# Products with tokens on partitions: 512 weight columns per matmul in place of 256, and another split of the PSUM banks

## The chip, the cores and the metric

The kernel runs on one core of a Trainium2 chip. The metric is the device time of one execution in microseconds. The kernel before took 967.45 us, the median of 3 runs (966.94 to 969.56).

## The reference

Two small networks one after the other, on 256 tokens of width 1024, in float32: x is 256 x 1024. Each layer is a normed mixer, added to x; the first network's two layers also have a SwiGLU feed-forward (width 2816) and a gated per-layer embedding. The four mixers are gated linear attention (GLA), differential attention (diff), a short convolution (conv) and block attention (MoBA). What the change touches are the input products of three of them:

```python
q, k, v, r, zf, zb = split_cols(h @ w_in, [512, 512, 1024, 1024, 16, 16])   # GLA
q, k, v = split_cols(h @ w_in, [1024, 1024, 1024])                          # diff
q, k, v, z = jnp.split(h @ w_in, 4, axis=-1)                                # MoBA, 1024 each
```

In diff and MoBA each head's q and k are normed over 64 columns (and turned by rotary angles in diff), then come scores, softmax and the product with v. The weights of all layers together are some 159 MB in float32, and each is read once.

## The kernel before, in words

**A stream of units.** All large products are one list of 315 units. A unit is a piece of 128 x 1024 weight elements: four k-tiles of 128 rows by 256 columns. SyncE loads it (`load`, L140 to L146), ScalarE rounds it to a high part `whi` (`high`, L152), VectorE subtracts to the low part `wlo` (`low`, L161), and TensorE multiplies. Each product of two float32 numbers is three matmuls, high x high, high x low and low x high (`mm3`, L205 to L208), so a unit of four k-tiles is 4 x 2 x 3 = 24 matmuls of 128x256. Loading and splitting run up to four units ahead of the products (`ahead`, `AHEAD`).

**Two ways round.** In most products the weights are the stationary side, 128 columns at a time, and x, 256 tokens, moves. In GLA's v and in q, k, v of diff and MoBA (`natural=True` in `gemm`, L210 to L236) the tokens are stationary, 128 at a time, and 256 columns of weights move, so that tokens come out on partitions.

**Sums and banks.** PSUM has 8 banks. A chunk of 256 columns sums into one bank (`bank`, tag g): 3 banks rotate. Small products (scores, transposes, attention outputs; `pm`, tag m) have the other 5 (L99, L100).

**The order.** `turn` walks through the units. The rest of the work, evacuations and small products, is queued by `at` and `chain` for a slot to come, a slot being a unit; the delays are in the table `DL` (L58 to L81). A chunk is evacuated `done` = 2 slots after its last unit. In the units' order `woven` lets two chunks (three in the mixers' output products) take turns at the head of a stage. Diff's order is q0 and k0 woven, q1, k1, q2, k2, v0, q3, k3, v1, v2, v3 in chunks of 256 columns (L1014); in MoBA q0 and k0 woven, q1, k1, v0, q2, k2, v1, q3, k3, v2, v3, z (L1229). The output products (`out_chunks`) are four chunks, the first three woven, and `add_h` (L371) adds a finished chunk to h on VectorE.

**Lines that the steps touch.** GLA: queries L584 and a scan's transposes L600 to L606, scores L633, states L651. x of a layer comes in four pairs of k-tiles, high part L284 (ScalarE) and low part L288 (VectorE). Diff: `qk_done` evacuates q and k with the rotary angles (L868, L873), `head_rms` norms (L775 to L781), `trans_split` transposes (L798) and splits (L803, L809); `scores` makes a product (L206 to L208 into m), its maximum (L921, L923), exponentials (L931), a mix (L948), transposes (L955), and the product with v (L976). Feed-forward: L462 to L475.

Of the kernel before, what the change touches and what calls it, by code (L numbers as in the profile page):

```python
# [19 lines left out]
P = 128  # L20
# [30 lines left out]
for _name, _n in (("ident", 128), ("dmask", 64)):  # L51
# [5 lines left out]
# Slots between a stage and the one before it (or the start of the phase); name.i is for its instance i.  # L57
# [14 lines left out]
    "dtu": 2, "dtu.2": 1.25, "dto": 0.75, "dpv.0": 5, "dpv.1": 7, "dpv.2": 3.25, "dpv.3": 0.75, "dosq": 0,  # L72
# [8 lines left out]
}  # L81
# What runs on GpSimd instead of VectorE
# [5 lines left out]
def body(ctx: ExitStack, tc: tile.TileContext, a, out: bass.AP):  # L88
# [10 lines left out]
    psg = ctx.enter_context(tc.tile_pool(name="psg", bufs=3, space=PSUM))  # L99
    psm = ctx.enter_context(tc.tile_pool(name="psm", bufs=5, space=PSUM))  # L100
# [13 lines left out]

    def bank():
        return psg.tile([P, 2, T], F32, tag="g", name="g")
# [4 lines left out]
    def on(name, i=None):  # L121
        """The engine that adds or multiplies what lies in SBUF."""
        return nc.gpsimd if (f"{name}.{i}" in POOL or name in POOL) else nc.vector
# [9 lines left out]
    # ---------------------------------------------------------------- the stream of weights  # L133
    # A unit is up to four k-tiles of a chunk of columns. Units are loaded and split ahead of
    # their products; what other engines and small products do is queued for a unit to come.
# [47 lines left out]
    def chain(i, *steps):  # L183
        """Queues steps, each its delay after the one before."""
        t = 0.0
        for d, fn in steps:
            t += wait(d, i)
            at(t, fn)
# [21 lines left out]
    def gemm(pieces, xs, done, natural=False):  # L210
        """Units of one chunk of 256 columns, its k-tiles in pieces (array, index, k-tiles of units).
        ps[:, j] = W[:, 128 j:].T @ x, or, natural, ps[:, t] = x[:, 128 t:].T @ W. One bank
        takes both sums: its first product clears it for the two."""
        total = sum(sum(u) for _, _, u in pieces)
        box, units, base = {}, [], 0
        for key, j, sizes in pieces:
            k0 = 0
            for kn in sizes:

                def fn(ks, kk=base + k0, kn=kn):  # L220
                    if kk == 0:
                        box["ps"] = bank()
                    ps = box["ps"]
                    for k, (wh, wl) in enumerate(ks):
                        xh, xl = xs[kk + k]
                        for s in range(2):
                            c = slice(s * P, (s + 1) * P)
                            ops = (xh[:, c], xl[:, c], wh, wl) if natural else (wh[:, c], wl[:, c], xh, xl)
                            mm3(ps[:, s], *ops, s + kk + k == 0, kk + k == total - 1, skip_group_check=True)
                    if kk + kn == total:  # L230
                        at("done", lambda: done(ps))

                units.append(((key, j, k0, kn, 256), fn))
                k0 += kn
            base += k0
        return units  # L236

    HALVES, TAIL = (4, 4), (4, 2, 2)

    def woven(chunks, n=2):  # L240
        """The first chunks take turns: their first k-tiles are there before the last."""
# [3 lines left out]
    # ---------------------------------------------------------------- small things  # L245
# [16 lines left out]
    def rsq(o, i, scale, bias, shape, nm):  # L262
        """o = (i * scale + bias) ** -0.5"""
# [81 lines left out]
    # the mixers', feed-forwards' and embeddings' norms in their order, and what they read  # L345
# [5 lines left out]
    def give(p, i, h):  # L351
        """Pair i of what norm p, or, last, the output, reads."""
# [14 lines left out]
    def add_h(p, i, ps, rb=None):  # L367
        """Pair i of hs[p + 1] = hs[p] + rb * ps"""
# [24 lines left out]
    # ---------------------------------------------------------------- per-layer embeddings  # L393
# [60 lines left out]
    # ---------------------------------------------------------------- feed-forward  # L454
# [35 lines left out]
    # ---------------------------------------------------------------- gated linear attention  # L490
    def gla_plan():
# [35 lines left out]
        def parts(d, hh):  # L527
            """max(-y, 0) and |y| of the gates y"""
# [19 lines left out]
        def scan(d):  # L548
            """b: 16 times the cumulated losses, less than nothing the logs of the decays, of the chunks"""
# [7 lines left out]
        def ends():  # L557
            """of the backward pass, what is left of the chunk from a token on"""
# [6 lines left out]
        def decay(d):  # L565
# [4 lines left out]
            # decays of whole chunks, and of tiles of two  # L570
# [21 lines left out]
        def far(d):  # L592
            """keys of the tile whose state the other tile reads, decayed to its end"""
# [123 lines left out]
        def chunk(j, done, natural=False):  # L717
            return gemm([("gla_i", j, (2, 2, 4) if j == 0 else HALVES)], xs, done, natural)

        units = [(("gla_z", 0, 4 * i, 4, 96), lambda ks, i=i: z_fn(ks, i)) for i in range(2)]  # L720
        for j in range(4):
            units += chunk(j, lambda ps, j=j: qk_done(ps, j % 2, j < 2))
        for j in range(4):
            units += chunk(4 + j, lambda ps, j=j: v_done(ps, j), True)
        for j in range(4):
            units += chunk(8 + j, lambda ps, j=j: r_done(ps, j))
# [41 lines left out]
    # ---------------------------------------------------------------- heads  # L768
    def head_rms(nm, N, src, out):
        """Steps to out.r = (mean square of 64 + eps / rn ** 2) ** -0.5 per token, tile and unit of 64."""  # L770
# [19 lines left out]
    def trans_split(nm, new, src, done, scale=None):  # L790
        """Steps: src() [tokens, 2 tiles, 256] -> hi, lo [128, 2 column tiles, 256 tokens], given to done"""
# [25 lines left out]
    def units64(t):  # L817
        return t.rearrange("p t (u c) -> p (t u) c", c=64)

    def per64(r):  # L820
        return r.rearrange("p t u -> p (t u)")[:, :, None].to_broadcast([P, 8, 64])

    # ---------------------------------------------------------------- differential attention
    def diff_plan():
# [40 lines left out]
        def qk_done(ps, i, nm):  # L865
# [3 lines left out]
            m2v = m2.rearrange("p t (u s c) -> p (t u) s c", s=2, c=32)  # L869
            pw = ps.rearrange("p t (u s c) -> p (t u) s c", s=2, c=32)  # L870
            tv = S.tabs[nm, "sin"].rearrange("p x (u s c) -> p (x u) s c", s=2, c=32)
            for s in range(2):
                nc.vector.tensor_mul(m2v[:, :, s], pw[:, :, 1 - s], tv[:, :, s])  # L873
# [32 lines left out]
        def scores(h):  # L906
# [38 lines left out]
            def mix():  # L945
                """l0 * (softmax of the first - lambda * softmax of the second)"""
# [58 lines left out]
        def q(i):  # L1005
            return gemm([("diff_i", i, HALVES)], N.xs, lambda ps: qk_done(ps, i, "q"), True)

        def k(i):
            return gemm([("diff_i", 4 + i, HALVES)], N.xs, lambda ps: qk_done(ps, i, "k"), True)

        def v(i):
            return gemm([("diff_i", 8 + i, HALVES)], N.xs, lambda ps: v_done(ps, i), True)

        units = woven([q(0), k(0), q(1), k(1), q(2), k(2), v(0), q(3), k(3), v(1), v(2), v(3)])  # L1014
# [11 lines left out]
    # ---------------------------------------------------------------- short convolution  # L1026
# [71 lines left out]
    # ---------------------------------------------------------------- block attention  # L1098
    def moba_plan():
# [122 lines left out]
        def chunk(j, done, natural=True):  # L1222
            return gemm([("moba_i", j, HALVES)], N.xs, done, natural)

        q = [chunk(i, lambda ps, i=i: qk_done(ps, i, "q")) for i in range(4)]
        k = [chunk(4 + i, lambda ps, i=i: qk_done(ps, i, "k")) for i in range(4)]
        v = [chunk(8 + i, lambda ps, i=i: v_done(ps, i)) for i in range(4)]
        z = [chunk(12 + i, lambda ps, i=i: z_done(ps, i), False) for i in range(4)]
        units = woven([q[0], k[0], q[1], k[1], v[0], q[2], k[2], v[1], q[3], k[3], v[2], v[3]] + z)  # L1229
# [44 lines left out]
def _cols(w, groups):  # L1274
    """[K, M] -> [len(groups), 128, K/128 * columns]: the groups' columns, K on partitions."""
# [12 lines left out]
def _part(v):  # L1288
    """[n * 128] -> [128, n]"""
# [30 lines left out]
def _arrays(i):  # L1320
# [48 lines left out]
    r["gla_i"] = _cols(w, _run(0, 3072))  # L1369
# [7 lines left out]
    r["diff_i"] = _cols(f["diff_w_in"][0], _run(0, 3072))  # L1377
# [5 lines left out]
    r["moba_i"] = _cols(f["attn_w_in_2"][0], _run(0, 4096))  # L1383
# [17 lines left out]
```

## Time and profile before

| what | value |
|---|---|
| median of 3 runs | 967.45 us |
| the profiled execution, span | 967.1 us |
| TensorE busy | 947.0 us (98%) |
| VectorE, ScalarE, GpSimd busy | 662.4, 557.0, 120.4 us |
| HBM read | 158.81 MB, 165 GB/s over the span |

Times are microseconds. PE is TensorE's matmul, PEld its weight load, DVE VectorE, ACT ScalarE, POOL GpSimd. A matmul is pipelined: its duration runs from its start to its modelled end and is longer than the time until the next one starts. In a timeline a row gives the start, the duration, the engine, the line, the operation, output<-inputs with their shape, how many are in the row, and in brackets how long the engine stood before it and what ended that.

### The profile page before, as it was taken

The numbers are of one execution on the slowest core, as the hardware profiler recorded it, in microseconds if no ns is written. First come the engines' busy times: TensorE is split into PE (matmuls) and PEld (weight loads), VectorE is DVE, ScalarE is ACT, GpSimd is POOL, SyncE is SP. The second block draws the span as 40 slices with busy tenths as digits, with TensorE's granted clock in tenths as the row PEclk, the third lists the DMA queues.
The fourth block names the chain that finished last, engine by engine and source line by source line (L and its number), as shares of the span: only waits on it lengthen the run. The fifth ranks groups of instructions, "written<-read, shape, count | busy, mean of one in ns | idle before, by whom it ended". The sixth has DMA issues, their size and how long they took to land.

```text
span 967.1 us, 19011 instructions
## 1 busy us (share of the span) xinstructions
PE 947.0 (98%) x7772; PEld 933.9 (97%) x7772; DVE 662.4 (68%) x988; ACT 557.0 (58%) x951; POOL 120.4 (12%) x85
## 2 busy tenths in 40 slices
PE   7999999999999989999999999999999999999998
PEld 6999999999999979999999999999999999999998
DVE  5883777656655698998685666565886667766663
ACT  6955666444444565676674454444774435677762
POOL 1060320000001452210010000012210003000010
PEclk9999999999999999999999999999999999999999
DMA  8543467655555644343565555565556536543332
GB/s 245 186 143 109 130 198 224 188 181 188 168 186 177 228 128 138 110 143 99 182 202 195 183 186 178 170 191 185 164 190 192 185 121 224 175 132 124 117 110 87
DMA packets 48008, 161.10 MB, mean 167 GB/s; under 512 B 5457, under 2 KB 6097, under 8 KB 47921
## 3 DMA queue, kind: packets, MB, share of 16 engines
q1 hardware_dynamic: 47376, 158.87, 51.7%
q8 instruction: 61, 1.00, 0.4%
q10 hardware_dynamic: 544, 1.02, 0.4%
q14 instruction: 27, 0.21, 0.1%
HBM read 158.81 MB, written 1.05 MB: 165 GB/s over the span
## 4 chain that ended last, share of the span: by engine, by line
PE 84%; DVE 7%; ACT 3%; DMA 2%; POOL 2%; issue 1%; SPq 0%; ACTq 0%; DVEq 0%; POOLq 0%
PE g L206 26%; PE g L207 25%; PE g L208 25%; DVE wlo L161 2%; ACT whi L152 1%; PE m L206 1%; DVE t L441 1%; PE m L798 1%; PE m L976 1%; DVE xl L288 1%; DMA h<-in_xT 1%; PE m L207 1%; PE m L1176 1%; DMA raw<-in_gla_i 1%; DMA raw<-in_ple_g 1%
## 5 line engine op out<-in xcount | busy, mean ns | idle before, releaser
L206 PE MATMUL g<-xh,whi 128*128 128x256 f32 (+1 forms) x1672 | 478.1, 286 | 6.4 <-ACT whi L152 6.2
L208 PE MATMUL g<-xh,wlo 128*128 128x256 f32 (+1 forms) x1672 | 475.0, 284 | 0.2 <-DVE wlo L161 0.2
L207 PE MATMUL g<-xl,whi 128*128 128x256 f32 (+1 forms) x1672 | 474.8, 284 | 0.1
L161 DVE TENSOR_TENSOR wlo<-raw,whi 128x1024 fp32r<-128x1024 f32 (+2 forms) x315 | 378.5, 1207 | 93.2 <-PE g L208 51.8
L152 ACT CAST whi<-raw 128x1024 fp32r<-128x1024 f32 (+2 forms) x315 | 312.0, 995 | 136.1 <-PE g L207 104.6
L206 PEld LDWEIGHTS g<-xh,whi 128*128 128x128 f32 (+1 forms) x1672 | 321.8, 192 | 7.8 <-ACT whi L152 6.6
L208 PEld LDWEIGHTS g<-xh,wlo 128*128 128x128 f32 (+1 forms) x1672 | 321.9, 192 | 1.0 <-DVE wlo L161 1.0
L207 PEld LDWEIGHTS g<-xl,whi 128*128 128x128 f32 (+1 forms) x1672 | 321.9, 193 | 0.9 <-DVE xl L288 0.6
L206 PE MATMUL g<-whi,xh 128*128 128x256 f32 x448 | 131.8, 294 | 2.7 <-ACT xh L284 2.7
L208 PE MATMUL g<-whi,xl 128*128 128x256 f32 x448 | 128.1, 286 | 1.8 <-DVE xl L288 1.8
L207 PE MATMUL g<-wlo,xh 128*128 128x256 f32 x448 | 128.0, 286 | 0.0
L206 PEld LDWEIGHTS g<-whi,xh 128*128 128x128 f32 x448 | 87.2, 195 | 4.1 <-ACT xh L284 2.9
L208 PEld LDWEIGHTS g<-whi,xl 128*128 128x128 f32 x448 | 87.0, 194 | 2.1 <-DVE xl L288 2.1
L207 PEld LDWEIGHTS g<-wlo,xh 128*128 128x128 f32 x448 | 87.3, 195 | 0.0
L474 ACT ACTIVATE t<-t 128x256 f32<-128x256 f32 x44 | 18.4, 418 | 96.2 <-DVE t L462 96.2
L207 PE MATMUL g<-al,whi 128*128 128x256 f32 x224 | 63.0, 281 | 0.0
L206 PE MATMUL g<-ah,whi 128*128 128x256 f32 x224 | 62.9, 281 | 0.0
L208 PE MATMUL g<-ah,wlo 128*128 128x256 f32 x224 | 62.9, 281 | 0.0
L462 DVE TENSOR_TENSOR t<-g,rb 128x256 f32<-128x256 f32 x44 | 18.6, 424 | 63.0 <-PE g L208 62.5
L362 POOL TENSOR_TENSOR h<-h,pj 128x512 f32<-128x512 f32 x8 | 12.4, 1559 | 294.6 <-DVE h L378 288.3
L304 POOL TENSOR_TENSOR acc<-acc,sq 128x512 f32<-128x512 f32 x16 | 28.8, 1800 | 149.5 <-ACT sq L297 125.2
L284 ACT ACTIVATE xh<-h,small 128x256 fp32r<-128x256 f32 x64 | 29.3, 502 | 30.7 <-POOL h L446 8.2
(219 smaller groups left out, 1009.8 us busy)
## 6 DMA issues: line engine op xcount, KB each, us to landing
raw<-in_ffn_i SPq DMA_DIRECT2D x88, 512.0 KB, 4.6
raw<-in_ffn_o SPq DMA_DIRECT2D x40, 512.0 KB, 4.0
raw<-in_conv_i SPq DMA_DIRECT2D x32, 512.0 KB, 4.6
raw<-in_moba_i SPq DMA_DIRECT2D x32, 512.0 KB, 4.4
raw<-in_diff_i SPq DMA_DIRECT2D x24, 512.0 KB, 3.8
raw<-in_gla_i SPq DMA_DIRECT2D x23, 512.0 KB, 5.3
raw<-in_ple_g SPq DMA_DIRECT2D x16, 512.0 KB, 4.7
raw<-in_gla_o SPq DMA_DIRECT2D x5, 512.0 KB, 3.8
```

Source lines behind the costliest of these rows:

```text
L152: nc.scalar.copy(hi[:, :kn * c], raws[u][:, :kn * c])
L161: nc.vector.tensor_sub(lo[:, :kn * c], raws.pop(u)[:, :kn * c], hi[:, :kn * c].bitcast(F32))
L206: nc.tensor.matmul(ps, lh, rh, start=first, stop=False, **kw)
L207: nc.tensor.matmul(ps, lh, rl, start=False, stop=False, **kw)
L208: nc.tensor.matmul(ps, ll, rh, start=False, stop=last, **kw)
L284: nc.scalar.activation(xh[:, j], h[:, j], AF.Copy, scale=gain[j])
L288: nc.vector.scalar_tensor_tensor(xl[:, j], h[:, j], gain[j], xh[:, j].bitcast(F32), op0=ALU.mult, op1=ALU.subtract)
L304: on("sqa", p).tensor_add(self.acc, self.acc, q)
L362: nc.gpsimd.tensor_add(n, h, proj[p // 3][i])
L441: on(f"pm{i // 3}", layer).tensor_mul(m[:, j], t[:, j], proj[layer][i][:, j])
L462: nc.vector.tensor_mul(g, ps[:, 0], N.rb)
L474: chain(layer, ("fs", lambda: nc.scalar.activation(sg, g, AF.Silu)), ("fm", lambda: nc.vector.tensor_mul(t3, sg, ps[:, 1])), ("fh", lambda ...
```

## The change

The products with tokens on partitions get a function of their own, `wide`. Its units are two k-tiles of 512 columns, the same 128 x 1024 elements, and 12 matmuls of 128x512 in place of 24 of 128x256. A wide chunk sums into a tile of two banks, one per 128 tokens. Its two halves of 256 columns are evacuated one after the other: the first 2 slots after the chunk's last unit, the second 2 slots later again (0.5 for v). The pool of sums is now two tiles of two banks, and ordinary chunks take the halves of such a tile in turn (`bank`); small products have 4 banks. The order of diff's units becomes q0, k0, q1, k1, v0, v1 in chunks of 512 columns, four units each, and in MoBA q0, k0, v0, q1, k1, v1, then z as before. Some delays of `DL` differ; views of q and k get a fourth dimension; the host lays the weights out in 512 columns.

```diff
-    psg = ctx.enter_context(tc.tile_pool(name="psg", bufs=3, space=PSUM))
-    psm = ctx.enter_context(tc.tile_pool(name="psm", bufs=5, space=PSUM))
+    psg = ctx.enter_context(tc.tile_pool(name="psg", bufs=2, space=PSUM))
+    psm = ctx.enter_context(tc.tile_pool(name="psm", bufs=4, space=PSUM))
...
+    halves = []
+
+    def banks():
+        return psg.tile([P, 2, 2 * T], F32, tag="g", name="g")
+
     def bank():
-        return psg.tile([P, 2, T], F32, tag="g", name="g")
+        if not halves:
+            g = banks()
+            halves.extend(g[:, i].rearrange("p (a b) -> p a b", b=T) for i in (1, 0))
+        return halves.pop()
...
+    def wide(key, j, xs, done, gap=2):
+        box, units = {}, []
+        for k0 in range(0, KT, 2):
+
+            def fn(ks, k0=k0):
+                if k0 == 0:
+                    halves.clear()
+                    box["ps"] = banks()
+                ps = box["ps"]
+                for k, (wh, wl) in enumerate(ks):
+                    xh, xl = xs[k0 + k]
+                    for t in range(2):
+                        c = slice(t * P, (t + 1) * P)
+                        mm3(ps[:, t], xh[:, c], xl[:, c], wh, wl, k0 + k == 0, k0 + k == KT - 1)
+                if k0 + 2 == KT:
+                    for i in range(2):
+                        at(wait("done") + gap * i, lambda i=i: done(ps[:, :, i * T:(i + 1) * T], 2 * j + i))
+
+            units.append(((key, j, k0, 2, 2 * T), fn))
+        return units
...
         for j in range(4):
-            units += chunk(4 + j, lambda ps, j=j: v_done(ps, j), True)
-        for j in range(4):
-            units += chunk(8 + j, lambda ps, j=j: r_done(ps, j))
+            units += chunk(4 + j, lambda ps, j=j: r_done(ps, j))
...
-        units = woven([q(0), k(0), q(1), k(1), q(2), k(2), v(0), q(3), k(3), v(1), v(2), v(3)])
+        q, k = [[wide("diff_i", 2 * n + j, N.xs, lambda ps, i, n=n, nm=nm: qk_done(ps, i - 4 * n, nm))
+                 for j in range(2)] for n, nm in enumerate("qk")]
+        v = [wide("diff_i", 4 + j, N.xs, lambda ps, i: v_done(ps, i - 8), 0.5) for j in range(2)]
+        units = q[0] + k[0] + q[1] + k[1] + v[0] + v[1]
...
-        units = woven([q[0], k[0], q[1], k[1], v[0], q[2], k[2], v[1], q[3], k[3], v[2], v[3]] + z)
+        units = q[0] + k[0] + v[0] + q[1] + k[1] + v[1]
...
-    "dtu": 2, "dtu.2": 1.25, "dto": 0.75, "dpv.0": 5, "dpv.1": 7, "dpv.2": 3.25, "dpv.3": 0.75, "dosq": 0,
+    "dtu": 1.25, "dto": 0.75, "dpv.0": 5.75, "dpv.1": 4.5, "dpv.2": 1.5, "dpv.3": 1.25, "dosq": 0,
```

The order of TensorE's instructions, at three places. In these rows g is a sum, m a small product's bank, and the number of a name is that of its tile; brackets name the engines that an instruction waits for.

The last two chunks of GLA's output product on TensorE, where the one ends and the other begins, before:

```order
L207 MATMUL g_1587<-xl_1308,whi_1488 128x256
L208 MATMUL g_1587<-xh_1307,wlo_1508 128x256
L206 MATMUL g_1587<-xh_1376,whi_1506 128x256 [waits Activation_49]
L207 MATMUL g_1587<-xl_1377,whi_1506 128x256
L208 MATMUL g_1587<-xh_1376,wlo_1526 128x256
```

These are two units of the last chunk, which has the bank g_1587 for itself. After:

```order
L215 MATMUL g_1322<-xh_1204,whi_1383 128x256
L216 MATMUL g_1322<-xl_1205,whi_1383 128x256
L217 MATMUL g_1322<-xh_1204,wlo_1403 128x256
L215 MATMUL g_1322<-xh_1272,whi_1401 128x256 [waits DVE_49,Activation_49]
L216 MATMUL g_1322<-xl_1273,whi_1401 128x256
```

Third and last chunk are halves of the tile g_1322, and the last chunk's second unit has a wait on VectorE beside the one on ScalarE.

The head of diff on TensorE, before, where the first unit of q0 (g_4286) ends and the first of k0 (g_4338) begins; xh_4195 and xh_4236 are the first two pairs of x:

```order
L206 MATMUL g_4286<-whi_4126,xh_4236 128x256
L207 MATMUL g_4286<-wlo_4164,xh_4236 128x256
L208 MATMUL g_4286<-whi_4126,xl_4237 128x256
L206 MATMUL g_4338<-whi_4162,xh_4195 128x256 [waits PE_49]
L207 MATMUL g_4338<-wlo_4205,xh_4195 128x256
```

After, where the fourth unit of q0 (g_4165), which reads the fourth pair xh_4226, ends and the first of k0 (g_4288) begins, with the norm's sum between:

```order
L215 MATMUL g_4165<-whi_4128,xh_4226 128x512
L216 MATMUL g_4165<-wlo_4161,xh_4226 128x512
L217 MATMUL g_4165<-whi_4128,xl_4227 128x512
L354 MATMUL m_4272<-ssum_4197,ones_86 128x256 [waits DVE_49]
L359 MATMUL m_4274<-ones_86,ssum_4197 128x4 x2
L215 MATMUL g_4288<-whi_4159,xh_4075 128x512 [waits PE_49]
```

q0 runs through all four pairs of x before k0 begins.

Small products in the middle of diff on TensorE, before: the transposes of a rotated chunk (m_4762) between a head's scores (m_4736) and a unit of k1 (g_4693):

```order
L207 MATMUL m_4736<-kl_4608,qh_4567 128x256
L208 MATMUL m_4736<-kh_4607,ql_4568 128x256
L798 MATMUL m_4762<-const_85,ro_4615 128x128 [waits PE_49,Pool_49]
L798 MATMUL m_4762<-const_85,ro_4615 128x128 x3
L206 MATMUL g_4693<-whi_4509,xh_4313 128x256
```

After, transposes of a head's weights (m_4798) and of a rotated chunk (m_4806) at the end of k1 (g_4577), ahead of v0 (g_4841):

```order
L217 MATMUL g_4577<-whi_4519,xl_4227 128x512
L988 MATMUL m_4798<-const_85,e_4641 128x128 [waits DVE_49,Activation_49]
L988 MATMUL m_4798<-const_85,e_4641 128x128
L988 MATMUL m_4798<-const_85,e_4641 128x128 [waits DVE_49]
L988 MATMUL m_4798<-const_85,e_4641 128x128
L831 MATMUL m_4806<-const_85,ro_4631 128x128 [waits DVE_49,Activation_49,Pool_49]
L831 MATMUL m_4806<-const_85,ro_4631 128x128 x3
L215 MATMUL g_4841<-whi_4564,xh_4075 128x512 [waits Activation_49]
```

The transposes of a rotated chunk now also wait for VectorE and ScalarE, and v0's sum for ScalarE.

## Rows read from the trace of the kernel before

**Rows 1.** The page: busy time of TensorE; the chain that ended last, by engine.

```profile
PE 947.0 (98%) x7772; PEld 933.9 (97%) x7772; DVE 662.4 (68%) x988; ACT 557.0 (58%) x951; POOL 120.4 (12%) x85
...
PE 84%; DVE 7%; ACT 3%; DMA 2%; POOL 2%; issue 1%; SPq 0%; ACTq 0%; DVEq 0%; POOLq 0%
```

**Rows 2.** The page's costliest groups: matmuls with weights moving, one kind of three.

```profile
L206 PE MATMUL g<-whi,xh 128*128 128x256 f32 x448 | 131.8, 294 | 2.7 <-ACT xh L284 2.7
```

**Rows 3.** Timeline of TensorE in MoBA, matmuls (PE) and weight loads (PEld).

```profile
846.05 0.28 PE L208 MATMUL g<-whi,xl 128*128 128x256 f32 x1
846.06 0.19 PEld L206 LDWEIGHTS g<-whi,xh 128*128 128x128 f32 x1
846.17 0.28 PE L206 MATMUL g<-whi,xh 128*128 128x256 f32 x1
```

**Rows 4.** Timeline of TensorE, a head's scores in MoBA.

```profile
848.23 0.27 PE L207 MATMUL m<-kl,qh 64*128 64x128 f32 x1
848.34 0.27 PE L208 MATMUL m<-kh,ql 64*128 64x128 f32 x1
```

**Rows 5.** Timeline of TensorE in diff, a stall and the matmuls behind it.

```profile
399.17 0.38 PE L207 MATMUL m<-kl,qh 64*128 64x256 f32 x1 [1.36 <-DVE kl L809]
...
401.74 0.41 PE L206 MATMUL g<-whi,xh 128*128 128x256 f32 x1
401.95 0.41 PE L207 MATMUL g<-wlo,xh 128*128 128x256 f32 x1
402.17 0.41 PE L208 MATMUL g<-whi,xl 128*128 128x256 f32 x1
```

**Rows 6.** Timeline of TensorE, four state products; then that line's durations (min/median/max).

```profile
70.60 1.02 PE L651 MATMUL m<-v,kn 128*128 128x256 f32 x4
...
L651 PE MATMUL m<-v,kn x16: 377/379/379, 70.6 to 93.5; 128*128 128x256 f32 x16
```

**Rows 7.** Timeline of TensorE in GLA's V units, its two waits.

```profile
59.41 0.66 PE L606 MATMUL m<-const,t 128*128 128x128 f32 x4 [0.23 <-POOL t L600]
...
61.40 0.59 PE L633 MATMUL m<-q,kk 128*128 128x192 f32 x2 [1.01 <-POOL q L584]
```

**Rows 8.** Windows: length, busy time of each engine, granted clock, DMA share, GB/s.

```profile
359.50:366.30 6.80, 4.73 (x20) 4.44 (x21) 6.50 (x11) 3.55 (x6) 1.33 (x1) 0.50 0.54 169
400.50:403.90 3.40, 3.40 (x18) 3.40 (x17) 3.29 (x8) 1.26 (x6) 0.00 (x0) 0.50 0.52 133
...
57.00:62.00 5.00, 3.76 (x29) 3.26 (x28) 5.00 (x4) 3.74 (x6) 4.92 (x4) 1.00 0.39 125
374.00:440.00 66.00, 64.64 (x533) 62.67 (x533) 64.15 (x133) 44.07 (x106) 12.47 (x10) 0.97 0.41 127
...
843.00:904.00 61.00, 61.00 (x494) 57.32 (x493) 40.43 (x77) 43.31 (x112) 0.00 (x0) 1.00 0.40 126
```

**Rows 9.** Timeline of TensorE at the head of diff.

```profile
359.76 0.58 PE L206 MATMUL g<-whi,xh 128*128 128x256 f32 x1 [2.66 <-ACT xh L284]
...
362.37 0.58 PE L208 MATMUL g<-whi,xl 128*128 128x256 f32 x1 [1.81 <-DVE xl L288]
```

**Rows 10.** Timelines of VectorE and TensorE at the end of GLA's output product.

```profile
134.69 0.68 DVE L371 TENSOR_TENSOR h<-g,h 128x512 f32<-128x512 f32 x1
...
133.45 0.28 PE L206 MATMUL g<-xh,whi 128*128 128x256 f32 x1
```

**Rows 11.** Timelines of VectorE and TensorE in the first feed-forward.

```profile
178.74 0.41 DVE L475 TENSOR_TENSOR t<-t,g 128x256 f32<-128x256 f32 x1
...
179.95 0.28 PE L206 MATMUL g<-xh,whi 128*128 128x256 f32 x1
```

**Rows 12.** Groups by line of VectorE and of ScalarE, 368 to 441 us.

```profile
L921 DVE TENSOR_REDUCE mx<-m 128x2 f32<-128x512 f32 x12 | 8.2, 682 | 0.2 <-PE m L208 0.2
...
L931 ACT ACTIVATE e<-m,nb,rqs 128x256 f32<-128x256 f32 x24 | 13.2, 562 | 7.4 <-DVE nb L923 6.9 <-PE m L955 0.5
L931 ACT ACTIVATION_READ_ACCUMULATOR e<-m,nb,rqs 128x1 f32 x24 | 4.8, 200 | 0.0
```

More of the change, by code (lines that the diff above doesn't have):

```diff
@@ L208, in mm3, with gemm @@
         nc.tensor.matmul(ps, ll, rh, start=False, stop=last, **kw)
-    def gemm(pieces, xs, done, natural=False):
+    def gemm(pieces, xs, done):
         total = sum(sum(u) for _, _, u in pieces)
@@ L224, in fn @@
                     for k, (wh, wl) in enumerate(ks):
+                        assert kk + k in xs, (key, kk, k, now, sorted(xs), side)
                         xh, xl = xs[kk + k]
@@ L227, in fn @@
                             c = slice(s * P, (s + 1) * P)
-                            ops = (xh[:, c], xl[:, c], wh, wl) if natural else (wh[:, c], wl[:, c], xh, xl)
-                            mm3(ps[:, s], *ops, s + kk + k == 0, kk + k == total - 1, skip_group_check=True)
+                            mm3(ps[:, s], wh[:, c], wl[:, c], xh, xl, s + kk + k == 0, kk + k == total - 1,
+                                skip_group_check=True)
                     if kk + kn == total:
@@ L715, in r_done, with chunk @@
             chain(h, ("grs", lambda: nc.scalar.activation(rr, rr, AF.Silu)), ("grm", mul), ("grh", hi), ("grl", lo))
-        def chunk(j, done, natural=False):
-            return gemm([("gla_i", j, (2, 2, 4) if j == 0 else HALVES)], xs, done, natural)
+        def chunk(j, done):
+            return gemm([("gla_i", j, (2, 2, 4) if j == 0 else HALVES)], xs, done)
         units = [(("gla_z", 0, 4 * i, 4, 96), lambda ks, i=i: z_fn(ks, i)) for i in range(2)]
@@ L722, in gla_plan @@
             units += chunk(j, lambda ps, j=j: qk_done(ps, j % 2, j < 2))
+        for j in range(2):
+            units += wide("gla_v", j, xs, v_done, 0.5)
         for j in range(4):
-            units += chunk(4 + j, lambda ps, j=j: v_done(ps, j), True)
-        for j in range(4):
-            units += chunk(8 + j, lambda ps, j=j: r_done(ps, j))
+            units += chunk(4 + j, lambda ps, j=j: r_done(ps, j))
         units += proj_u + out_chunks("gla_o", S.og, 0)
@@ L817, in units64 @@
     def units64(t):
-        return t.rearrange("p t (u c) -> p (t u) c", c=64)
+        return t.rearrange("p t (u c) -> p t u c", c=64)
     def per64(r):
-        return r.rearrange("p t u -> p (t u)")[:, :, None].to_broadcast([P, 8, 64])
+        return r[:, :, :, None].to_broadcast([P, 2, 4, 64])
     def diff_plan():
@@ L868, in qk_done @@
             nc.vector.tensor_mul(m1, ps, S.tabs[nm, "cos"].rearrange("p (t h) c -> p t (h c)", t=2))
-            m2v = m2.rearrange("p t (u s c) -> p (t u) s c", s=2, c=32)
-            pw = ps.rearrange("p t (u s c) -> p (t u) s c", s=2, c=32)
-            tv = S.tabs[nm, "sin"].rearrange("p x (u s c) -> p (x u) s c", s=2, c=32)
+            m2v = m2.rearrange("p t (u s c) -> p t u s c", s=2, c=32)
+            pw = ps.rearrange("p t (u s c) -> p t u s c", s=2, c=32)
+            tv = S.tabs[nm, "sin"].rearrange("p (t x) (u s c) -> p t (x u) s c", t=2, s=2, c=32)
             for s in range(2):
-                nc.vector.tensor_mul(m2v[:, :, s], pw[:, :, 1 - s], tv[:, :, s])
+                nc.vector.tensor_mul(m2v[:, :, :, s], pw[:, :, :, 1 - s], tv[:, :, :, s])
             def add():
@@ L1003, in pv @@
                   *trans_split("do", new_x, lambda: b.n, ready, S.gs))
[L1005 to L1012, printed above, removed]
-        units = woven([q(0), k(0), q(1), k(1), q(2), k(2), v(0), q(3), k(3), v(1), v(2), v(3)])
+        q, k = [[wide("diff_i", 2 * n + j, N.xs, lambda ps, i, n=n, nm=nm: qk_done(ps, i - 4 * n, nm))
+                 for j in range(2)] for n, nm in enumerate("qk")]
+        v = [wide("diff_i", 4 + j, N.xs, lambda ps, i: v_done(ps, i - 8), 0.5) for j in range(2)]
+        units = q[0] + k[0] + q[1] + k[1] + v[0] + v[1]
         units += proj_u + out_chunks("diff_o", S.og, 3)
@@ L1220, in z_done @@
             chain(i, ("mzs", lambda: nc.scalar.activation(rr, rr, AF.Silu)), ("mzm", mul), ("mzh", hi), ("mzl", lo))
[L1222 to L1228, printed above, removed]
-        units = woven([q[0], k[0], q[1], k[1], v[0], q[2], k[2], v[1], q[3], k[3], v[2], v[3]] + z)
+        q, k = [[wide("moba_i", 2 * n + j, N.xs, lambda ps, i, n=n, nm=nm: qk_done(ps, i - 4 * n, nm))
+                 for j in range(2)] for n, nm in enumerate("qk")]
+        v = [wide("moba_i", 4 + j, N.xs, lambda ps, i: v_done(ps, i - 8), 0.5) for j in range(2)]
+        units = q[0] + k[0] + v[0] + q[1] + k[1] + v[1]
+        for i in range(4):
+            units += gemm([("moba_z", i, HALVES)], N.xs, lambda ps, i=i: z_done(ps, i))
         units += out_chunks("moba_o", S.og, 7)
@@ L1368, in _arrays @@
     w = f["gla_w_in"][0]
-    r["gla_i"] = _cols(w, _run(0, 3072))
+    r["gla_i"] = _cols(w, _run(0, 1024) + _run(2048, 3072))
+    r["gla_v"] = _cols(w, _run(1024, 2048, 512))
     r["gla_z"] = _cols(w, [[(3072, 3104)] * 3])
@@ L1376, in _arrays @@
     r["gla_o"] = _cols(f["gla_w_out"][0], _run(0, D))
-    r["diff_i"] = _cols(f["diff_w_in"][0], _run(0, 3072))
+    r["diff_i"] = _cols(f["diff_w_in"][0], _run(0, 3072, 512))
     r["diff_o"] = _cols(f["diff_w_out"][0], _run(0, D))
@@ L1382, in _arrays @@
     r["conv_o"] = _cols(f["conv_w_out_2"][0], _run(0, D))
-    r["moba_i"] = _cols(f["attn_w_in_2"][0], _run(0, 4096))
+    r["moba_i"] = _cols(f["attn_w_in_2"][0], _run(0, 3072, 512))
+    r["moba_z"] = _cols(f["attn_w_in_2"][0], _run(3072, 4096))
     r["moba_o"] = _cols(f["attn_w_out_2"][0], _run(0, D))
```

6 rows, old and new, of the table DL are left out of this document.

## The prediction

> **What bounds the kernel now.** I read the page first, then the timeline of single matmuls, the windows by stage, and last the timelines around the places where TensorE stood. The page says that TensorE is busy for 947.0 of 967.1 us and carries 84% of the chain that ended last [rows 1]. So nearly everything is the sum of matmul steps, and the 20 us that are left are a start and a few stalls. The change touches the 1344 matmuls of 128x256 whose moving side is weights: 448 rows of each of three kinds, of which one kind is shown [rows 2].
>
> The timeline gives their step, which the mean duration (294 ns, pipelined) hides: starts at 846.05 and 846.17, which is 120 ns a matmul (so it goes on for whole units), and a weight load begins 0.01 us after the matmul before it has started [rows 3]. At 2.4 GHz, 256 columns stream in 107 ns, so 13 ns of a step are something else. A 64x128 product, half the columns, steps hardly faster: 848.23 to 848.34 [rows 4]. So short matmuls sit on a floor of 110 to 120 ns that does not go with columns. At the low clock the same 256 columns step by 0.21 us (401.74, 401.95, 402.17), which is 256 columns at 1.2 GHz with nothing on top [rows 5]. I take from this that the load, not the streaming, sets the 120 ns, and that it hides under anything longer.
>
> **A 512-column matmul.** None is in the trace. Its nearest row is the state product of line 651: 256 fp32 columns at two passes stream as long as 512, with new weights each time. Four of them take 1.02 us and one 379 ns, so they step by (1020 - 379)/3 = 214 to 217 ns [rows 6]. I take 216. The bounds: 213, bare streaming, and 227, if the 13 ns are paid once per matmul whatever its length. One wide step replaces two of 120: 240 - 216 = 24 ns by 672 matmuls is 16.1 us gross, 0.29 us per unit (12 wide steps, 2.59 us, for 24 narrow, 2.88 us): 2.3 us over GLA's 8 units, 6.9 over diff's 24, 6.9 over MoBA's 24.
>
> The Trainium skill, page "TensorE: Matmul & The Clock Gate", section "Back-to-back issue gap", speaks against this: its table for matmuls by themselves has 262 cycles for 256 columns and 518 for 512, which is 109 and 216 ns. By it a pair would save 2.5 ns, and all of them 1.7 us. The rows agree with it on the long matmul and not on the short one, which steps by 120 [rows 3].
>
> **GLA's V, +0.9 us.** TensorE does not end this stage alone: after six of the eight V units it waits at 59.41 and again at 61.40 for GpSimd, 1.24 us in all [rows 7]. GpSimd's work does not get faster, so the 6 x 0.29 = 1.7 us of those units only lengthen the wait, to 3.0 us; two units keep 0.6. Then the clock: 1.24 us of idle left it at full, 57 to 62 [rows 8], but after the idle of 1.36 at 399.17 the matmuls from 400.50 to 403.90 went at half [rows 5, 8], and after 2.66 and 1.81 us at 359.76 and 362.37 so did the stretch to 366.3 [rows 8, 9]. A half-clock stretch of 3.40 us costs 3.40 x (1 - 120/213) = 1.5 us. I take it as lost here: -0.6 + 1.5. Bounds -2.3 and +1.5.
>
> **The last chunks of GLA's output product, +3.4 us.** Two chunks of ordinary products now share one two-bank tile, and the order shows TensorE's first product of the second chunk behind a wait on VectorE that was not there. VectorE adds the first chunk to h from 134.69 for 0.68 us; TensorE began the second chunk at 133.45 [rows 10]. So it now stands 135.37 - 133.45 = 1.9 us, and I count the clock's 1.5 as lost. Bounds: 0, if VectorE comes as much earlier, and 3.4. The same sharing is in every second chunk of the feed-forwards, but there the evacuation (178.74 for 0.41) ends 0.8 us before the unit's start (179.95) [rows 11]: nothing. If VectorE slips by a microsecond in one of those, it shows as a wait.
>
> **Diff, -4.5 us.** First its start. TensorE stood 2.66 us for the fourth pair of x, and 1.81 for its low part at 362.37 [rows 9]. By then 62 of the 96 narrow products of q0 and k0 were done (two units, half a third, and two). In the new order q0 runs through alone: three units of 12 wide products and two more are done by then, as much as 76 narrow ones. The 14 more, at 107 ns, are 1.5 us; for this I count the first three units (0.9) as spent. Then VectorE: between 374 and 440 it is busy 64.15 of 66.00 us [rows 8]. Some 17 units lie there, and of their 4.9 us only the 1.85 us of VectorE's slack can come out. The other four units keep 1.2. The stall of 1.36 us on the low part of k [rows 5] I leave, with its clock: VectorE makes it, and what the four small banks add takes the place of what order would free. A bank of scores is held by a reduce of 682 ns and two rounds of exponentials of 562 + 200 [rows 12], 2.2 us, nearly a whole unit; with four of them rather than five, and half the evacuations of q and k a slot or two later, TensorE's next score product meets the reader more often, as the order's waits show. Bounds: -10 (all 6.9, the extra 0.6, the stall 1.36 and its 1.5) and +6.5 (below).
>
> **MoBA, -5.9 us.** VectorE is busy 40.43 and ScalarE 43.31 of 61 us between 843 and 904 [rows 8]; neither presses, so the 24 units keep their 6.9 us. The last heads are now scored under the z units; one wait as long as the one seen at 61.40, 1.0 us [rows 7], goes off. Bounds -6.9 and -3.
>
> DMA: units are as many and as large as before (128x1024 each), and a stream that is 0.29 us a unit quicker asks for a tenth more from a share that is 0.40 between 843 and 904 [rows 8]: nothing. The four-dimensional views of the rotary step move as many elements: nothing.
>
> **Sum.** +0.9 + 3.4 - 4.5 - 5.9 = -6.1 us. The profiled execution spans 967.1 us, 0.35 below the median of 967.45, so 961.0 becomes **961.4 us**.
>
> **Rivals.**
> - *The waits don't bite.* Clock kept in GLA and in its output product (-3.0), diff at its TensorE bound (-5.5), MoBA without its wait (-1.0): 951.9 us. For it, VectorE is free outside diff; against it, the 97% of VectorE inside.
> - *A fixed load.* If the 13 ns stay on a 512-column matmul, a pair saves 13 and not 24: GLA's 0.6 becomes 0.3, MoBA's 6.9 becomes 3.8, diff loses 1.2: 966.0 us. For it, a load stands before each matmul at any length; against it, the half-clock step without anything on top [rows 5] and line 651 [rows 6].
> - *The columns are the price.* If both lengths stream without a gap and the 120 ns is something that wide matmuls pay in proportion, a pair gains 1 to 2 ns. Then GLA gives 1.5, its output 3.4, diff 0 but for the order (-0.6), MoBA +0.3: +4.6, 972 us. The table of the Trainium skill's page "TensorE: Matmul & The Clock Gate" comes to the same.
> - *Slower: TensorE locked to VectorE and ScalarE.* In diff two sum tiles alternate, the second half of a chunk is read only four slots after its end, just before the tile is wanted again, and four small banks rotate. By the readers in the order I count some 11 places, over the last half of diff's units, where a product takes a bank whose reader stands close before it. It decides when these waits are about 1 us each, which a chain of 2.2 us allows: +11 us in place of none, 972.4 us; from 0.55 us a place on the change gains nothing. For it, VectorE at 97%; against it, in the trace of before TensorE's waits in that part sum to 1.36 us [rows 5].
>
> **How the numbers follow.** About 0.3% (2.9 us) can be told from no change. Forecast 0.50, its own range 956.5 to 966; waits don't bite 0.17; fixed load 0.13; columns 0.06; locked 0.14. Faster (below 964.5): 0.47 of the forecast, all of the second, 0.02 of the third: 0.66. Same: 0.03, 0.10 and 0.03 of the locked: 0.16. Slower: the rest, 0.18. The range runs from 952 to 971, which leaves out half of the case at 951.9 and most of the two at 972.
>
> **What would show it.** In the profile after: 224 wide matmuls of each kind, with starts 0.216 us apart at full clock (0.227: fixed load; 0.238: columns). A wait of about 3 us on GpSimd near 59 us and of about 2 on VectorE near 133, each with a low clock behind it. MoBA's 24 units shorter by about 6 us. In diff, from the first wide unit to the output product, about 4.5 us less, VectorE at 97% or more, and TensorE's waits on small banks. I am wrong if the wide step is right and diff still grows, or if the ordinary chunks, the feed-forwards above all, show waits on VectorE that I put at nothing.

## The result and the profile after

The changed kernel takes 1064.8 us (median of 4 runs, 1061.9 to 1075.89) against 967.55 us before in the same comparison: a ratio of 1.102, interval 1.096 to 1.107. It is 10% slower. The prediction was 961.4, with a range of 952 to 971. The profiled execution spans 1059.2 us, 92.1 more than the one before.

The page of the changed kernel, busy time of each engine and the chain that ended last:

```profile
PE 960.8 (91%) x7100; PEld 908.2 (86%) x7100; DVE 653.1 (62%) x988; ACT 559.9 (53%) x955; POOL 120.1 (11%) x85
...
PE 75%; DVE 10%; ACT 7%; DMA 3%; issue 2%; POOL 1%; SPq 0%; ACTq 0%; POOLq 0%; DVEq 0%
```

Against [rows 1], TensorE has 672 instructions less and is busy 13.8 us longer, and it now stands for 98 us (1059.2 - 960.8) where it stood for 20. VectorE and ScalarE do as much as before. So it is a matter of waits, and of matmuls that run slower behind some of them (mean granted clock 0.984, before 0.993). What TensorE waits for, by the wait view of the changed kernel (us in total, times, longest):

```profile
PE g L215 <- DVE t L508: 39.6, 20, 2.0
PE g L215 <- ACT whi L161: 8.4, 2, 6.1
PE g L215 <- DVE u L1067: 7.4, 7, 1.1
PE g L215 <- DVE t L408: 4.4, 5, 0.9
PE g L215 <- DVE h L404: 3.8, 2, 3.0
...
PE g L215 <- ACT v L936: 2.8, 1, 2.8
PE m L1203 <- DVE sc L1178: 2.5, 1, 2.5
PE m L1009 <- DVE t L1028: 2.4, 1, 2.4
PE m L1203 <- ACT pr L1197: 2.4, 3, 1.5
PE g L215 <- DVE n L1146: 2.3, 1, 2.3
PE m L1219 <- ACT aT L1207: 2.1, 1, 2.1
PE m L831 <- ACT e L964: 2.0, 1, 2.0
PE g L215 <- ACT t L808: 1.9, 1, 1.9
...
PE m L215 <- ACT e L964: 0.4, 1, 0.4
```

The largest is on L508, the feed-forward's gate product (L475 in the kernel before). The feed-forwards have no wide matmul. The start of each stage's first large matmul, taken from the two traces, gives the time per stage. The last three columns are three of the experiments below, by stage from their traces:

| stage (us in the profile) | before | after | difference | alternate halves | banks alone | narrow in the wide order |
|---|---|---|---|---|---|---|
| GLA's input products, embedding | 107.1 | 108.8 | +1.7 | 112.5 | 111.2 | 106.2 |
| GLA's output product | 23.0 | 27.5 | +4.5 | 24.8 | 23.0 | 23.0 |
| feed-forwards, input, both | 254.3 | 300.5 | +46.3 | 257.6 | 307.1 | 256.1 |
| feed-forwards, output, both | 125.6 | 129.9 | +4.4 | 125.6 | 135.2 | 125.6 |
| gates, both | 46.9 | 52.2 | +5.3 | 47.6 | 54.4 | 46.9 |
| diff with its output product | 136.1 | 142.6 | +6.5 | 148.1 | 135.6 | 145.1 |
| convolution with its output | 116.5 | 126.3 | +9.8 | 132.4 | 122.6 | 116.5 |
| MoBA with z and output | 147.2 | 161.1 | +13.8 | 159.7 | 153.6 | 158.1 |

Of the 92 us, 70 lie in stages whose matmuls the change doesn't touch at all: GLA's output, the feed-forwards, the gates and the convolution. They share only the banks. The other 22 lie where the wide matmuls are.

**A wide matmul** steps by 227 ns. MoBA, timeline of TensorE with its weight loads, changed kernel:

```profile
896.72 0.39 PE L215 MATMUL g<-whi,xh 128*128 128x512 f32 x1
896.95 0.39 PE L216 MATMUL g<-wlo,xh 128*128 128x512 f32 x1
897.17 0.39 PE L217 MATMUL g<-whi,xl 128*128 128x512 f32 x1
897.40 0.39 PE L215 MATMUL g<-whi,xh 128*128 128x512 f32 x1
...
896.95 0.19 PEld L217 LDWEIGHTS g<-whi,xl 128*128 128x128 f32 x1
897.18 0.19 PEld L215 LDWEIGHTS g<-whi,xh 128*128 128x128 f32 x1
```

From 896.72 to 897.40 are three steps of 0.227 us: 512 columns at 2.4 GHz are 213 ns, and the 13 ns on top are as many as 256 columns have [rows 3]. A wide matmul in place of two narrow ones saves 13 ns, not 24, a unit 0.16 us, and the gross gain is 672 x 13.3 = 8.9 us, not 16.1.

**A feed-forward's stall**, timelines of the changed kernel, VectorE and TensorE of one pair of chunks:

```profile
204.16 0.28 PE L217 MATMUL g<-xh,wlo 128*128 128x256 f32 x1
204.48 0.42 DVE L495 TENSOR_TENSOR t<-g,rb 128x256 f32<-128x256 f32 x1 [4.53 <-PE g L217]
204.82 1.22 DVE L170 TENSOR_TENSOR wlo<-raw,whi 128x1024 fp32r<-128x1024 f32 x1
204.99 0.42 ACT L507 ACTIVATE t<-t 128x256 f32<-128x256 f32 x1 [5.34 <-DVE t L495]
...
205.95 0.41 DVE L508 TENSOR_TENSOR t<-t,g 128x256 f32<-128x256 f32 x1
...
206.42 0.38 PE L215 MATMUL g<-xh,whi 128*128 128x256 f32 x1 [1.98 <-DVE t L508]
```

And the same place before, VectorE:

```profile
177.27 0.42 DVE L462 TENSOR_TENSOR t<-g,rb 128x256 f32<-128x256 f32 x1 [1.65 <-PE g L208]
177.61 1.22 DVE L161 TENSOR_TENSOR wlo<-raw,whi 128x1024 fp32r<-128x1024 f32 x1
178.74 0.41 DVE L475 TENSOR_TENSOR t<-t,g 128x256 f32<-128x256 f32 x1
```

Read the two side by side. The three VectorE instructions are the same and take the same 1.9 us. Before, they begin when TensorE has finished the chunk, and end 0.8 us before TensorE's next unit but one [rows 11]. In the changed kernel VectorE has stood for 4.53 us, and begins 0.04 us after the end of a TensorE unit (204.44). Counting the matmuls from the stage's start says which: the chunk that is scaled was finished at 201.56, and the unit that ends at 204.44 is the first of the pair's *second* chunk. Both chunks lie in one tile. That is one unit, 2.88 us, later than before. The 0.8 us of margin become 0.80 - 2.88 = -2.1, and TensorE, whose second unit in that tile waits in turn for the gate product, stands 1.98 us. There are 11 pairs in each feed-forward. That VectorE waits because of the shared tile is put to the test below.

**GLA's output product**, the wait that was forecast:

```profile
138.19 0.55 PE L215 MATMUL g<-xh,whi 128*128 128x256 f32 x1 [2.96 <-DVE h L404]
```

And the window behind it (length, busy time of PE, PEld, DVE, ACT, POOL, granted clock, DMA share, GB/s), with the clock at half:

```profile
138.20:140.00 1.80, 1.80 (x8) 1.80 (x9) 1.38 (x3) 1.80 (x4) 0.72 (x2) 0.50 0.67 241
```

### The profile page after: what moved, and what is told of

It is laid out like the page before. It is cut to its first block, busy times and chain, and to the rows that moved or that the text cites. A ratio compares the mean times of both kernels' runs of the same rounds, so it can differ in the third digit from the quotient of the medians.

```text
span 1059.2 us, 17686 instructions
## 1 busy us (share of the span) xinstructions
PE 960.8 (91%) x7100; PEld 908.2 (86%) x7100; DVE 653.1 (62%) x988; ACT 559.9 (53%) x955; POOL 120.1 (11%) x85
## 3 DMA queue, kind: packets, MB, share of 16 engines
q1 hardware_dynamic: 47376, 158.87, 46.3%
## 4 chain that ended last, share of the span: by engine, by line
PE 75%; DVE 10%; ACT 7%; DMA 3%; issue 2%; POOL 1%; SPq 0%; ACTq 0%; POOLq 0%; DVEq 0%
PE g L215 24%; PE g L216 23%; PE g L217 23%; DVE wlo L170 4%; ACT whi L161 2%; PE m L1009 1%; DMA graw<-in_gla_g 1%; ACT xh L317 1%; DMA raw<-in_ple_g 1%; DVE t L508 1%; PE m L831 1%; DVE xl L321 1%; DMA raw<-in_moba_i 1%; DVE t L474 1%; DMA h<-in_xT 1%
## 5 line engine op out<-in xcount | busy, mean ns | idle before, releaser
L215 PE MATMUL g<-xh,whi 128*128 128x256 f32 (+1 forms) x1672 | 484.4, 290 | 68.7 <-DVE t L508 39.6
L215 PE MATMUL g<-whi,xh 128*128 128x512 f32 x224 | 92.8, 414 | 4.2 <-DVE n L1146 2.3
L216 PE MATMUL g<-wlo,xh 128*128 128x512 f32 x224 | 89.1, 398 | 0.0
L217 PE MATMUL g<-whi,xl 128*128 128x512 f32 x224 | 88.9, 397 | 0.1
L215 PEld LDWEIGHTS g<-whi,xh 128*128 128x128 f32 x224 | 43.1, 192 | 14.2 <-DVE n L1146 2.6
L217 PEld LDWEIGHTS g<-whi,xl 128*128 128x128 f32 x224 | 43.2, 193 | 10.1 <-DVE xl L321 0.5
L216 PEld LDWEIGHTS g<-wlo,xh 128*128 128x128 f32 x224 | 43.3, 193 | 8.0
```

Of the source, the lines that this page charges most:

```text
L215: nc.tensor.matmul(ps, lh, rh, start=first, stop=False, **kw)
L216: nc.tensor.matmul(ps, lh, rl, start=False, stop=False, **kw)
L217: nc.tensor.matmul(ps, ll, rh, start=False, stop=last, **kw)
```

## The experiments

Spans are of profiled executions; us are medians.

### Neighbouring chunks in different tiles

```diff
     def bank():
-        if not halves:
-            g = banks()
-            halves.extend(g[:, i]... for i in (1, 0))
-        return halves.pop()
+        turns[0] += 1
+        mine = halves[turns[0] % 2]
+        if not mine:
+            mine.extend(pair())
+        return mine.pop()
```

(`pair` makes the two halves; `wide`, the embedding's products and an output product begin with fresh tiles.)

> The change, with one thing undone: neighbouring ordinary chunks take halves of different two-bank tiles (first tile's first half, second tile's first half, first tile's second half, and so on), so that a chunk's evacuation no longer lies behind the next chunk's first unit. Theory A (the tile of two banks is tracked as one; VectorE's read of a finished first half waits for TensorE's first unit in the second half, and TensorE's second unit there waits for VectorE, about 2.0 us a pair of chunks): the 20 waits on the feed-forward's gate product (39.6 us) and those of the convolution (7.4 us) go, each feed-forward's input goes from 150 us back to 127, the whole falls by 60 to 75 us to 990 to 1005. Theory B (the four small banks and the wide chunks' waits, or a lower clock everywhere, are the cause): it falls by less than 15 us.

Measured: 1021.6 us, ratio to before 1.056 (1.054 to 1.057), 43 us below the change. The waits on the gate product fall from 39.6 us to 2.5:

```profile
PE g L223 <- DVE t L1108: 7.0, 3, 2.9
PE g L223 <- DVE t L553: 6.9, 1, 6.9
...
PE g L223 <- DVE t L520: 2.5, 2, 1.3
```

VectorE's scaling again waits 1.65 us, as before the change, and comes a unit earlier:

```profile
209.00 0.42 DVE L507 TENSOR_TENSOR t<-g,rb 128x256 f32<-128x256 f32 x1 [1.65 <-PE g L225]
209.34 1.22 DVE L178 TENSOR_TENSOR wlo<-raw,whi 128x1024 fp32r<-128x1024 f32 x1
210.47 0.41 DVE L520 TENSOR_TENSOR t<-t,g 128x256 f32<-128x256 f32 x1
```

The feed-forwards' inputs take 257.6 us, where the change took 300.5 and the kernel before 254.3, and their outputs are back. That is theory A, for these stages. But its number for the whole, 990 to 1005, is missed: the convolution is worse than in the change (132.4 for 126.3, waits of 7.0 us on L1108), GLA's first part too (6.9 us on L553), diff is 5.6 us longer still (148.1), and MoBA nearly as slow as it was (159.7). A chunk now ties up the tile of the next but one, which would fit sums that are read late; this was not tried apart. So the remedy has a price of its own, and something else is at work in diff and MoBA.

### The banks alone, and the four small banks alone

```diff
-    psg = ... name="psg", bufs=3
-    psm = ... name="psm", bufs=5
+    psg = ... name="psg", bufs=2
+    psm = ... name="psm", bufs=4
...
+            halves.extend(g[:, i]... for i in (1, 0))
```

(in the kernel before, with `banks` and `bank` of the change), and

```diff
-    psm = ... name="psm", bufs=5
+    psm = ... name="psm", bufs=4
```

> The kernel before, narrow matmuls and its own order of units, with only the banks of the change: ordinary chunks take the halves of a two-bank tile in turn, four small banks. Theory A: slower by 60 to 100 us, with the same 20 waits of about 2 us in the feed-forwards. Theory B (wide matmuls or their order are the cause): within 15 us of the kernel before.

> The kernel before with four banks for small products in place of five, and nothing else (one bank lies idle). Theory A: 0 to +6 us, in diff and MoBA alone, as five banks are rarely all held. Theory B (small banks are a main cause): +15 us or more.

Measured: the banks alone, in one run, 1055.1 us, a span of 1053.3 and so 86 us over the one before, without one wide matmul. The waits of TensorE there:

```profile
PE g L214 <- DVE t L483: 44.2, 22, 2.3
...
PE g L214 <- ACT t L783: 5.8, 5, 2.2
```

22 waits on the gate product, 2.0 us each. Four small banks alone: 968.03 against 967.89, ratio 1.0005 (0.9995 to 1.0015), nothing. So what costs the feed-forwards their time is the two-bank tile under ordinary chunks, and neither the wide matmul nor the smaller pool. By stage (table above) the banks alone leave diff where it was and cost MoBA 6.4 us; there q, k and v are ordinary chunks that share tiles, which the changed kernel's wide chunks don't. GLA's output doesn't wait in this run, because other chunks pair up there: its third and last chunk lie in different tiles.

### Narrow matmuls in the wide order

```diff
-        units = woven([q(0), k(0), q(1), k(1), q(2), k(2), v(0), q(3), k(3), v(1), v(2), v(3)])
+        units = [u for f, n in ((q, 0), (k, 0), (q, 2), (k, 2), (v, 0), (v, 2)) for u in woven([f(n), f(n + 1)])]
...
-        units = woven([q[0], k[0], q[1], k[1], v[0], q[2], k[2], v[1], q[3], k[3], v[2], v[3]] + z)
+        units = [u for n in (0, 2) for c in (q, k, v) for u in woven(c[n:n + 2])]
```

(with the change's delays, its evacuation slots, four one-bank sums and four small banks)

> The kernel before with its narrow matmuls, one-bank sums (four of them) and four small banks, but with q, k and v of diff and MoBA in the order and with the evacuation slots that the wide chunks give them (pairs of 256-column chunks woven, done a slot or two later, the change's delays). Theory C (the coarse chunks, not the matmuls, cost the rest: heads come in two bursts, the last of them too late to be covered by the stream): diff to its output product +6 to +14 us, MoBA's z units and output +8 to +14 us, with the waits on scores, transposes and exponentials that the change shows at the z units; 985 to 993 us in all. Rival D (the two-bank sum tiles are the rest too, also in diff and MoBA): within 4 us of the kernel before.

Measured: 989.6 us in one run, span 987.7. Everything outside diff and MoBA stands within 2 us of before; diff with its output is +9.0, MoBA with z and output +10.9 (table above). z takes 43.48 us in this run, and 43.46 in the changed kernel. The waits of TensorE in this run:

```profile
PE m L1176 <- DVE sc L1151: 2.5, 1, 2.5
PE m L976 <- DVE t L995: 2.4, 1, 2.4
...
PE m L1192 <- ACT aT L1180: 2.1, 1, 2.1
```

They are those of the changed kernel at the same lines (L1203 on L1178, 2.5; L1009 on L1028, 2.4; L1219 on L1207, 2.1). What the windows of z say, before and in this run (length, PE, PEld, DVE, ACT, POOL, clock, DMA share, GB/s):

```profile
908.20:939.60 31.40, 31.40 (x267) 29.56 (x265) 20.45 (x33) 24.70 (x54) 4.13 (x3) 1.00 0.38 118
```

```profile
915.00:958.50 43.50, 38.89 (x283) 35.42 (x282) 23.17 (x47) 32.94 (x75) 2.57 (x2) 0.92 0.20 69
```

Before, TensorE is never idle under z. With the wide order more of the heads' work is there (47 VectorE instructions for 33, 75 of ScalarE for 54), TensorE stands for 4.6 us of 43.5, and the clock is at 0.92. Four units of q and four of k must pass before a head can begin, where two and two did, and then two groups come at once. Counted in the traces, the scores of 12 of MoBA's 16 heads are made before z and 4 under it in the kernel before; in this run and in the changed kernel it is 8 and 8. That is theory C. Rival D, which had this run within 4 us of the kernel before, is out. What the run doesn't separate is the order, the slots and delays that go with it, and the four small banks: some of its waits, as L976 on L995, are of a product that takes a small bank whose reader isn't done. The wide order with five small banks, or with other delays, was not tried.

What the wide matmuls themselves gave in these stages is small. With the order taken as given, diff's stages are 2.5 us shorter in the change than in this run (142.6 for 145.1), and MoBA's 3.0 longer (161.1 for 158.1), where 48 units by 0.16 us would be 7.7. Part of it stands in the waits of the changed kernel for a tile of sums that is still being read (2.33 us for MoBA's norm, L1146, and 1.88 for diff's square, L808, at the start of a wide chunk; 2.75 for diff's v, L936, behind the last one). That this is all of it was not tried.

### The gate product ahead of the split

```diff
-"fm": 0.5
+"fm": 0
```

> The change, with the feed-forward's gate product moved ahead of the next split of weights on VectorE (its delay 0 in place of half a slot). Theory A says what makes up one of the 2.0 us stalls: after TensorE's first unit in the shared tile, VectorE's scaling (0.42), then a split of weights (1.22) that hides ScalarE's silu, then the gate product (0.41). Without the split the chain is 0.42 + 0.42 + 0.41 and the handing over, 1.4 us: each of the 22 stalls falls by 0.5 to 0.7 us, 11 to 15 us in all, 1047 to 1054 us. Rival: the stall is the wait for the split weights or for a bank, and stays at 2.0 us a pair.

Measured: 1050.3 us in one run, inside the expected 1047 to 1054. The change's own runs lie 14 us apart, so the profiled executions are the better pair: 1048.5 for 1059.2, 10.7 less, a little under the expected 11 to 15. VectorE and the wait view of this run:

```profile
204.12 0.42 DVE L495 TENSOR_TENSOR t<-g,rb 128x256 f32<-128x256 f32 x1 [4.53 <-PE g L217]
205.08 0.42 DVE L508 TENSOR_TENSOR t<-t,g 128x256 f32<-128x256 f32 x1 [0.54 <-ACT t L507]
205.42 1.22 DVE L170 TENSOR_TENSOR wlo<-raw,whi 128x1024 fp32r<-128x1024 f32 x1
```

```profile
PE g L215 <- DVE t L508: 29.9, 20, 1.8
```

The wait for TensorE's unit stays (4.53), and the stall shrinks from 1.98 to 1.5 us with the chain behind it. The 20 waits lose 9.7 us, which is most of the 10.7. That VectorE's chain behind the wait sets the stall is shown.

### Wide matmuls in the order of before

```diff
-        units = woven([..., v(1), v(2), v(3)])
+        units = woven([..., v(1), wide("diff_v", 0, N.xs, vv_done)])
...
+                    box["ps"] = [psg.tile([P, 2 * T], F32, tag="g", name="g") for _ in range(2)]
```

(a bank per 128 tokens, evacuated each by itself; four one-bank sums, four small banks, one delay in diff half a slot longer; the same for MoBA's v, and in the first of the two runs for GLA's v)

> The kernel before with four small banks and four one-bank sums, and wide matmuls only where order and slots stay as they were: GLA's v (8 units) and the last two chunks of v in diff and in MoBA (4 units each), with a bank of its own for each 128 tokens and evacuation by token halves (diff's third product with v half a slot later). If a wide step is 227 ns, as the change's trace shows, a unit is 0.16 us shorter: diff and MoBA together give 1.3 us, GLA's up to 1.3, of which its wait for GpSimd may take most: 965 to 966.5 us. If the wide matmul itself brings new stalls, it is slower than before by 1 us or more.

> The run before this with wide v, without its GLA part: wide matmuls only in the last two chunks of v of diff and of MoBA (8 units), one bank per 128 tokens, four small banks. In the run with GLA's v wide too, diff to its output product stood 1.3 us shorter and MoBA 0.4, while the stage behind GLA's v was 1.7 us longer, TensorE waiting for v's evacuation. Theory: the 227 ns step gives its 1.3 to 1.7 us once nothing hangs on the wide chunk: 966 to 967.5 us, ratio 0.998 to 0.9995. Rival: the small gains are lost elsewhere, ratio 1.000 or more.

Measured: with GLA's v 968.83 against 968.75, ratio 1.0003 (0.9993 to 1.0013); without it 967.63 against 968.24, ratio 1.000 (0.9991 to 1.001). Neither is faster by what can be told. In the profile of the first, the stage behind GLA's v is 1.74 us longer, with a new wait there:

```profile
PE m L671 <- ACT v L648: 1.3, 1, 1.3
```

v's second half comes in one piece, and the states wait for it. What the wide units give can't be read from single stages. Four of them should save 0.64 us. Against the kernel before, MoBA is 0.44 us shorter in the first run and 0.41 longer in the second. Diff to the end of its output is 1.25 and 0.67 shorter, but it is 0.53 shorter with four small banks and no wide matmul, too. The expectation of 965 to 966.5 us is missed. In the second run 967.63 lies 0.1 us above the expected range; its interval holds both no gain and the upper end of the expected ratio, 0.9995, so a gain below 0.9 us is not excluded. No version run here beats the kernel before.

## Why the prediction was wrong, point by point

- **The same sharing in the feed-forwards: "nothing".** This is the step that failed. The prediction saw that two chunks share a tile and that TensorE's second unit there waits for VectorE. It then took VectorE's time from the trace of before (178.74 for 0.41, 0.8 us ahead of the unit [rows 11]) as if it stayed there. But the tie goes both ways: VectorE's first read waits for TensorE's unit in the other half. The evacuation moves a whole unit back, and the margin is -2.1 us. With 22 pairs that is +46 us in the feed-forwards' inputs alone; the gates (+5.3), the feed-forwards' outputs (+4.4) and the convolution (+9.8) have the same pairs. Waits on VectorE in the feed-forwards were one of the signs by which the prediction said it would know itself wrong.
- **GLA's output product, +3.4.** Measured +4.5. The wait was forecast at 1.9 us and is 2.96; behind it the matmuls run at half clock (0.50), so the forecast loss of the clock was there too. The wait is longer for the same reason as in the feed-forwards: VectorE itself came later, since its first add there, at 130.95, had stood 1.60 us for TensorE, where it had stood 0.16 at 127.89 before. (What the prediction calls TensorE's start of the second chunk, 133.45, is the start of the last chunk's second unit, the one with the new wait; the sum is the same.)
- **A 512-column matmul, 216 ns.** Measured 227, the upper bound: the rival of a fixed load. Line 651 misled: its step of 214 to 217 has hardly anything on top of what 512 columns take, and why is open. The gross gain is 8.9 us. The table of the Trainium skill's page "TensorE: Matmul & The Clock Gate", section "Back-to-back issue gap", has 518 cycles for 512 columns of a matmul by itself, 216 ns, and 262 for 256, 109 ns; in this kernel's stream the trace shows 227 and 120.
- **GLA's V, +0.9.** The stages of v and r together came to +1.1 (-1.35 and +2.4), near the number by luck. The eight units gave 8 x 0.16 = 1.3; the wait for GpSimd stayed at 1.00 us instead of growing to 3.0, and the clock that was counted as lost stayed at 1.00 behind it. Instead a wait for v's own evacuation (1.1 us, the states at L684) came, and one of 0.8 us for a sum of r that VectorE still reads (L734).
- **Diff, -4.5.** Measured +6.5. The start came out better than thought: there is no stall at its head. But VectorE was taken as the bound, and with 49.83 us of 56 and then 33.88 of 45 (windows below) it is none any more. From 440 us to the output product TensorE stands five times, 9.4 us in all: behind L964 twice, L808, L1028 and L936 (waits above). None of these lines makes an input of the product that waits; each reads a bank on ScalarE or VectorE. The prediction had set such waits off against a stall of 1.36 us. That the heads come later and in bursts was in the order of units, and no term stood for it; with narrow matmuls, the wide order with its slots, delays and four small banks costs 9.0.

The windows of diff in the changed kernel, its first part and its last (columns as above):

```profile
384.00:440.00 56.00, 54.80 (x277) 44.50 (x275) 49.83 (x98) 34.70 (x73) 19.17 (x13) 1.00 0.50 155
440.00:485.00 45.00, 39.47 (x206) 32.64 (x207) 33.88 (x79) 27.92 (x71) 6.45 (x4) 0.89 0.27 88
```

- **MoBA, -5.9.** Measured +13.8; the wide order with its slots, delays and four small banks makes 10.9 by itself. The sentence that failed: one wait of 1.0 us for the last heads under z. There are five of TensorE's waits under z in the changed kernel, 5.6 us in all, and the clock over z is 0.96.
- **The rival on the slower side** had the right kind of cause, TensorE locked to VectorE and ScalarE, and in diff nearly the right size: it priced the waits on banks there at 11 us, where 9.4 were measured, about half of them on small banks and half on sums. That diff ended at +6.5, just where it put it, is luck, as the start came out better. It had nothing for the other 86 us. Four small banks cost nothing in the order of before; what a fifth would save in the wide order was not tried.

## What to carry to other kernels

When a change makes two things share a tile, follow the new waits in both directions: who now waits for the writer of the other half, and from when on; a margin read off the old trace is void as soon as its earlier end has a new wait. Count it over every user of the resource, not in the stages that the change is about: a pool is shared by all. And a coarser unit of work that saves 6% of its own time can cost more than that, if side work that it feeds begins later and comes in bursts: here some 20 us (989.6 for 967.9) with the same matmuls.

## What the runs showed of the hardware

In these streams, where every matmul has new weights, a step is 13 ns longer than its columns take at full clock (2.4 GHz), for 256 and for 512 of them (120 and 227 ns), though the next weights are loaded from the start of the matmul on. At half clock (1.2 GHz) 256 columns step by 0.21 us, with nothing on top [rows 5], and 512 by 0.43, where the columns alone take 427 ns. In the changed kernel, behind a wait in diff, granted clock 0.50 in this stretch:

```profile
444.37 0.63 PE L217 MATMUL g<-whi,xl 128*128 128x512 f32 x1
444.80 0.63 PE L215 MATMUL g<-whi,xh 128*128 128x512 f32 x1
445.23 0.63 PE L216 MATMUL g<-wlo,xh 128*128 128x512 f32 x1
```

Why the cost shows at full clock alone is open.
